# Two small table transfers moved from SyncE's queue to ScalarE's in a rotary-embedding kernel

## The chip, the cores and the metric

The kernel runs on one core of a Trainium2 chip. The metric is device time in microseconds (us), the median over executions. Ratios of two kernels are computed as the mean time of one kernel's fast runs over that of the other's of the same rounds, so they are not quite the ratio of the medians that are quoted beside them.

## The reference

```python
# x: [16, 512, 1024] float32, 16 heads of 64; cos, sin: [512, 32]
x = x.reshape(batch, seq, num_heads, head_dim)
x1, x2 = x[..., :32], x[..., 32:]
rotated = concatenate([x1 * cos - x2 * sin, x1 * sin + x2 * cos], axis=-1)
```

The input and the output are 33.55 MB each; the two tables are 64 KB each. There is little arithmetic for each byte.

## The kernel before

The batch is cut into eight tiles of 4 MB, each with 128 partitions of 8 x 1024 elements (eight slices "k" of 1024). Five tiles are held on chip at once. SyncE issues every transfer, in program order:

```python
FIRST = (3, 8)              # where the first tile's load is cut: k 0-2, then k 3-7
LAST_OUT = (4, 8)           # the last tile's store, likewise
...
    load(0, 0, FIRST[0])
    sin_sb = bp.tile([P, dim], FP32, name="b")[:PB, : KK * half]
    cos_sb = bp.tile([P, dim], FP32, name="b")[:PB, : KK * half]
    nc.sync.dma_start(out=sin_sb, in_=sin_v)
    nc.sync.dma_start(out=cos_sb, in_=cos_v)
    for lo, hi in zip(FIRST, FIRST[1:]):
        load(0, lo, hi)
    for t in range(1, BUFS):
        load(t)
```

PE then spreads the tables over 128 partitions, and VectorE (DVE in the profile) prepares them. Nothing of the main work can start earlier, because each main operation reads a table:

```python
    nc.tensor.matmul(out=sin_t, lhsT=spread, rhs=sin_sb, start=True, stop=True)   # L104
    nc.tensor.matmul(out=cos_t, lhsT=spread, rhs=cos_sb, start=True, stop=True)   # L105
    nc.vector.tensor_scalar_mul(out=sns[:, :, 0, :], in0=sin_k, scalar1=-1.0)     # L107
    nc.vector.tensor_copy(out=sns[:, :, 1, :], in_=sin_k)                         # L108
    ...
    for t in range(NT):            # main work: VectorE products and sums, GpSimd products,
        ...                        # PE and ScalarE for two of eight k
        nc.vector.tensor_tensor(out=pairs(ps), in0=pairs(rc), in1=cos_b(...), op=ALU.mult)  # L171
```

L171 is the first main operation of VectorE.

Of the kernel before, what the change touches and what calls it, by code (L numbers as in the profile page):

```python
# [27 lines left out]
def kernel(  # L28
# [13 lines left out]
    nc = tc.nc  # L42
# [12 lines left out]
    cos_v = cos.rearrange("(p k) j -> p (k j)", k=KK)  # L55
    sin_v = sin.rearrange("(p k) j -> p (k j)", k=KK)
# [22 lines left out]
    load(0, 0, FIRST[0])  # L79
    sin_sb = bp.tile([P, dim], FP32, name="b")[:PB, : KK * half]  # L80
    cos_sb = bp.tile([P, dim], FP32, name="b")[:PB, : KK * half]
    nc.sync.dma_start(out=sin_sb, in_=sin_v)
    nc.sync.dma_start(out=cos_sb, in_=cos_v)
    for lo, hi in zip(FIRST, FIRST[1:]):
        load(0, lo, hi)
    for t in range(1, BUFS):
# [27 lines left out]
    def cos_b(k, n):  # L114
        c = cos_t[:, k * half : (k + 1) * half]
        return bass.AP(tensor=c.tensor, offset=c.offset, ap=[c.ap[0], [0, n], [1, half]])
# [17 lines left out]
    def pairs(r):  # L134
        return r.rearrange("p (a j) -> p a j", j=half)
# [21 lines left out]
    for t in range(NT):  # L157
        xt = tiles[t]
        for k in range(KK):
# [6 lines left out]
            if k in PE_ROWS[t % 2]:  # L166
                parts = []
                for c in range(0, dim, BANK):
# [3 lines left out]
                        out=pairs(ps), in0=pairs(rc), in1=cos_b(k, BANK // half), op=ALU.mult  # L172
# [51 lines left out]
```

## Time and profile before

| | before |
|---|---|
| time, median of 3 runs | 162.77 us (162.58 to 162.78) |
| span of the profiled run | 160.8 us |
| VectorE busy | 141.4 us, 88% |
| transfers | 67.26 MB, packets on 97.9% of 16 engines' span |
| sine, cosine table: issue to landing | 6.5, 6.3 us |
| first main VectorE operation | at 10.90 us |
| last store issued | at 152.14 us |

Two rows compete for being the bound: VectorE, which never stops once it has started, and the transfers, which never stop at all.

### The profile page before, as it was taken

Reading aid. Unit: us, or ns where it says so; the run is one execution under the profiler, and the core shown is the slowest. Engines: PE = TensorE matmul, PEld = TensorE weight load, DVE = VectorE, ACT = ScalarE, POOL = GpSimd, SP = SyncE. Lnnn points to the kernel's source line nnn. Section 1 sums busy time; section 2 is a strip of 40 time slices with the busy share of each in tenths; the row PEclk is TensorE's granted clock in tenths of the full one; section 3 lists DMA queues with packets and bytes.
Section 4 is the critical chain, followed back from the end, with each engine's and each line's share of the span. In section 5 each row is a group of like instructions: output and inputs, shape, how many; then the busy total and the mean of one; then the engine's idle time right before and its main releaser. Section 6 shows DMA issues by size and latency. Waiting matters only on the chain. (4 is left out here: it accounts for less than half of the span.)

```text
span 160.8 us, 524 instructions
## 1 busy us (share of the span) xinstructions
PE 62.3 (39%) x71; PEld 20.0 (12%) x71; DVE 141.4 (88%) x142; ACT 20.0 (12%) x33; POOL 130.3 (81%) x62
## 2 busy tenths in 40 slices
PE   3045380546217260708035440918053721735000
PEld 0022020202011110202020200211020201111000
DVE  1059999999999999999999999999999999999800
ACT  0110220021102020111102020112002110202000
POOL 1039999999999999999999899999999799950000
PEclk9999958576956755595555555555955585587655
DMA  5999999999999999999999999999999999999994
GB/s 186 395 423 463 408 481 416 391 497 416 391 489 416 402 416 481 408 391 505 399 399 481 424 399 475 424 408 432 465 399 432 465 408 432 457 416 408 428 428 179
DMA packets 2754, 67.26 MB, mean 418 GB/s; under 512 B 320, under 2 KB 448, under 8 KB 448
## 3 DMA queue, kind: packets, MB, share of 16 engines
q1 hardware_dynamic: 2752, 67.24, 97.9%
q14 instruction: 2, 0.02, 0.0%
HBM read 33.69 MB, written 33.55 MB: 418 GB/s over the span
## 5 line engine op out<-in xcount | busy, mean ns | idle before, releaser
L165 POOL TENSOR_TENSOR b<-xt,sns 128x1024 f32<-128x1024 f32 x56 | 129.6, 2358 | 11.8 <-DVE sns L108 9.4
L183 DVE TENSOR_TENSOR pd<-xt,tab 128x1024 f32<-128x1024 f32 x48 | 58.1, 1225 | 0.8
L145 DVE TENSOR_TENSOR xt<-pd,b 128x1024 f32<-128x1024 f32 x48 | 58.4, 1218 | 0.0
L178 PE MATMUL ps<-xt,ident 128*128 128x512 f32 x32 | 29.5, 1077 | 48.6 <-issue 38.1
L178 PE MATMUL ps<-b,ident 128*128 128x512 f32 x32 | 29.4, 1073 | 29.8 <-DVE ps L171 27.1
L179 ACT COPY xt<-ps 128x512 f32<-128x512 f32 x32 | 18.7, 585 | 120.3 <-PE ps L178 120.3
L171 DVE TENSOR_TENSOR ps<-xt,tab 128x512 f32<-128x512 f32 x32 | 20.6, 688 | 0.0
L178 PEld LDWEIGHTS ps<-xt,ident 128*128 128x128 f32 x32 | 9.4, 324 | 68.2 <-issue 63.6
L178 PEld LDWEIGHTS ps<-b,ident 128*128 128x128 f32 x32 | 9.2, 316 | 49.7 <-issue 25.6
L176 DVE TENSOR_TENSOR xt<-xt,tab 128x1024 f32<-128x1024 f32 x8 | 9.8, 1221 | 0.4
L107 DVE TENSOR_SCALAR sns<-tab 128x256 f32<-128x256 f32 x1 | 0.4, 424 | 8.2 <-PE tab L105 8.2
L104 PE MATMUL tab<-b,spread 64*128 64x256 f32 x2 | 1.2, 696 | 5.1 <-DMA b<-in_sin_dram 5.1
L179 ACT ACT_TABLE_LOAD x1 | 1.3, 1283 | 7.3 <-DMA xt<-in_x_dram 7.3
L95 PE MATMUL ps<-zero 128*128 128x512 bf16 x3 | 1.5, 626 | 1.2 <-DVE zero L92 1.2
L104 PEld LDWEIGHTS tab<-b,spread 64*128 64x128 f32 x2 | 0.5, 307 | 6.0 <-issue 6.0
L105 PE MATMUL tab<-b,spread 64*128 64x256 f32 x2 | 1.1, 631 | 0.0
L92 DVE MEMSET zero<- 128x256 uint32 x1 | 0.3, 272 | 0.9 <-PEq L205 0.9
L105 PEld LDWEIGHTS tab<-b,spread 64*128 64x128 f32 x2 | 0.7, 333 | 0.2
L103 DVE COPY spread<-ident 64x64 f32<-64x64 f32 x2 | 0.3, 184 | 0.2 <-POOL ident masks.py:199 0.2
L95 PEld LDWEIGHTS <-zero 128*128 128x128 bf16 x3 | 0.3, 124 | 1.5 <-DVE zero L92 1.2
masks.py:197 POOL MEMSET ident<- 128x128 f32 x1 | 0.2, 205 | 0.3 <-POOLq L205 0.3
L108 DVE COPY sns<-tab 128x256 f32<-128x256 f32 x1 | 0.4, 414 | 0.0
(6 smaller groups left out, 0.9 us busy)
## 6 DMA issues: line engine op xcount, KB each, us to landing
xt<-in_x_dram SPq DMA_DIRECT2D x7, 4096.0 KB, 29.1
out_dram<-xt SPq DMA_DIRECT2D x7, 4096.0 KB, 23.6
out_dram<-xt SPq DMA_DIRECT2D x2, 2048.0 KB, 8.1
xt<-in_x_dram SPq DMA_DIRECT2D x1, 2560.0 KB, 11.5
xt<-in_x_dram SPq DMA_DIRECT2D x1, 1536.0 KB, 6.5
b<-in_sin_dram SPq DMA_DIRECT2D x1, 64.0 KB, 6.5
b<-in_cos_dram SPq DMA_DIRECT2D x1, 64.0 KB, 6.3
```

What stands on the lines that cost most here:

```text
L95: nc.tensor.matmul(out=ps, lhsT=zero[:, :P], rhs=zero, start=True, stop=True)
L104: nc.tensor.matmul(out=sin_t, lhsT=spread, rhs=sin_sb, start=True, stop=True)
L105: nc.tensor.matmul(out=cos_t, lhsT=spread, rhs=cos_sb, start=True, stop=True)
L107: nc.vector.tensor_scalar_mul(out=sns[:, :, 0, :], in0=sin_k, scalar1=-1.0)
L108: nc.vector.tensor_copy(out=sns[:, :, 1, :], in_=sin_k)
L145: nc.vector.tensor_tensor(out=r, in0=ps, in1=b, op=ALU.add)
L165: nc.gpsimd.tensor_tensor(out=halves(b), in0=swapped(r, nh), in1=over_heads(sk), op=ALU.mult)
L171: nc.vector.tensor_tensor(out=pairs(ps), in0=pairs(rc), in1=cos_b(k, BANK // half), op=ALU.mult)
L176: nc.vector.tensor_tensor(out=halves(r), in0=halves(r), in1=swapped_signed(k), op=ALU.mult)
L178: nc.tensor.matmul(out=ps, lhsT=ident, rhs=rhs, start=False, stop=True, skip_group_check=True)
L179: nc.scalar.copy(out=rc, in_=ps)
L183: nc.vector.tensor_tensor(out=pairs(ps), in0=pairs(r), in1=cos_b(k, 2 * nh), op=ALU.mult)
```

## The change

The intent is to free SyncE of two issues and to let the tables arrive on a queue of their own, beside the first piece of x instead of behind it.

```diff
-    nc.sync.dma_start(out=sin_sb, in_=sin_v)
-    nc.sync.dma_start(out=cos_sb, in_=cos_v)
+    nc.scalar.dma_start(out=sin_sb, in_=sin_v)
+    nc.scalar.dma_start(out=cos_sb, in_=cos_v)
```

Nothing else changes: the order of the other instructions is the same on each engine.

## The prediction

> **What bounds the kernel now.** I read the page's busy shares first, then the chain that ended last, then the transfers, because the first two and the third give different answers. VectorE (DVE) is the busiest compute engine, and the chain that ended last is made of its work:
>
> ```profile
> PE 62.3 (39%) x71; PEld 20.0 (12%) x71; DVE 141.4 (88%) x142; ACT 20.0 (12%) x33; POOL 130.3 (81%) x62
> ...
> DMA  5999999999999999999999999999999999999994
> ...
> q1 hardware_dynamic: 2752, 67.24, 97.9%
> ...
> DVE 10%; DVEq 1%; issue 1%
> ```
>
> That fits a VectorE bound: it starts late and then never stops. But the transfer row is at 9 from the second slice to the last but one, and the one queue's packets fill 97.9% of the time of 16 DMA engines. Two chains therefore run side by side over nearly the whole span. The table of windows shows which of them has room (columns: window, its length, busy time of PE, PEld, DVE, ACT, POOL with counts, granted clock, DMA share, GB/s):
>
> ```profile
> 0.00:1.50 1.50, 0.31 (x1) 0.13 (x2) 0.43 (x3) 0.00 (x0) 0.70 (x6) 1.00 0.00 0
> 1.50:2.50 1.00, 1.00 (x3) 0.15 (x1) 0.13 (x2) 0.00 (x0) 0.00 (x0) 1.00 1.06 209
> 2.50:20.00 17.50, 5.79 (x9) 2.34 (x8) 10.01 (x13) 2.45 (x3) 9.31 (x5) 1.00 0.99 415
> 20.00:60.00 40.00, 18.21 (x20) 5.67 (x20) 39.69 (x39) 5.85 (x10) 40.00 (x18) 0.68 1.01 433
> 60.00:100.00 40.00, 14.68 (x16) 4.71 (x16) 39.60 (x40) 4.68 (x8) 39.56 (x18) 0.54 1.00 433
> 100.00:140.00 40.00, 18.76 (x20) 5.87 (x20) 39.61 (x39) 5.60 (x10) 38.27 (x17) 0.59 1.00 433
> 140.00:150.00 10.00, 3.58 (x4) 1.17 (x4) 9.90 (x11) 1.42 (x3) 2.50 (x2) 0.83 0.98 424
> 150.00:158.00 8.00, 0.00 (x0) 0.00 (x0) 2.06 (x2) 0.00 (x0) 0.00 (x0) 0.51 1.00 430
> ```
>
> The DMA share is 0.98 to 1.06 in every window from 1.5 to 158 us, and the rate in the long windows is 433 GB/s each time, whether loads or stores are moving. The transfer engines have no hole to fill. As a check: 67.26 MB at 433 GB/s is 155.3 us; with 1.5 us before the first packet and about 2.8 us after 158 that is 159.6 of the 160.8 us span, and the slow first slices (186 and 395 GB/s) account for most of the missing 1.2 us. So **the transfers bound the kernel**, and VectorE keeps pace just behind them.
>
> How close is it? The last store, 2 MB, is issued when VectorE is done:
>
> ```profile
> 152.14 0.33 SPq L77 DMA_DIRECT2D out_dram<-xt  x1
> ...
> out_dram<-xt SPq DMA_DIRECT2D x2, 2048.0 KB, 8.1
> xt<-in_x_dram SPq DMA_DIRECT2D x1, 1536.0 KB, 6.5
> b<-in_sin_dram SPq DMA_DIRECT2D x1, 64.0 KB, 6.5
> b<-in_cos_dram SPq DMA_DIRECT2D x1, 64.0 KB, 6.3
> ```
>
> It lands at about 152.14 + 8.1 = 160.2 us. The first load (1536 KB, 1.57 MB, 3.6 us at 433 GB/s) met an empty queue and took 6.5 us, so start and landing cost some 2.9 us on an idle queue. A 2 MB store (2.10 MB, 4.8 us) would then take about 7.7 us on an idle queue; 8.1 leaves an estimated 0.4 us of backlog in front of it. VectorE is thus some 0.4 us ahead of running the queue dry at the end: balanced, with the transfers deciding.
>
> **What the Trainium skill says.** "DMA: Bandwidth & Descriptors", section "Issuing engines are not separate DMA queues": transfers from ScalarE and SyncE run on the same 16 engines and interleave; another issuer only saves the sequencer's issue time. The kernel before uses one queue, so its trace can't show the interleaving. The same page, "Queues, rings and completion order": each engine alternates between the rows it has work for, packet by packet, draining a packet of several descriptors before it switches. No run here shows that yet; it is why I expect the tables not to wait behind all of the queued loads. The same page, "Where 436 GB/s comes from", puts the ceiling at 435.2 GB/s; the 433 GB/s of the long windows agrees. "Perfetto Trace Analysis", section "DMA Instruction — HWDGE (DVE, Sync)": the profiled interval of such an instruction leaves out the movement of data. The trace agrees: 0.52 us of issue for the sine table, 6.5 us to landing.
>
> **The change part by part.** *Removed from SyncE:* two issues of 0.52 and 0.58 us. The next load is issued at 2.36 us now, about 1.2 us earlier after. Worth nothing: the first load's 1.57 MB keep the engines busy until past 5 us, so that load waits in the queue either way. *Added to ScalarE:* the same two issues, some 1.1 us, at the start. Its first work needs PE, at 15.79 us, so this costs nothing. No other engine's order changes, and bytes and packets stay the same.
>
> *Moved: when the tables land.* Today they lie in the queue behind the first load:
>
> ```profile
> 7.77 1.19 PE L104 MATMUL tab<-b,spread 64*128 64x256 f32 x2 [5.12 <-DMA b<-in_sin_dram]
> ...
> 9.85 0.42 DVE L107 TENSOR_SCALAR sns<-tab 128x256 f32<-128x256 f32 x1 [8.22 <-PE tab L105]
> ...
> 10.90 1.29 DVE L171 TENSOR_TENSOR ps<-xt,tab 128x512 f32<-128x512 f32 x2
> ```
>
> Sine lands at 1.17 + 6.5 = 7.7 us, cosine at 1.74 + 6.3 = 8.0, the first piece of x at 0.73 + 6.5 = 7.2. From the sine landing, four matmul passes and three VectorE operations take 3.2 us to the first real operation at 10.90. On a queue of their own the tables are issued at about 0.7 us; alternating with the first load I expect them by 4 to 6.5 us. The first piece of x then decides: at 7.2 us, plus up to 0.3 for the 0.13 MB of tables moved in front of its end. VectorE's main work starts at 7.5 to 9.5 us, my middle 8.0, about 3 us earlier. GpSimd gains less: its third operation needs the load issued at 2.36 us, which lands at 2.36 + 11.5 = 13.9 as before, so it waits there.
>
> *What of it reaches the end.* VectorE works without a break at 17.6 us a tile (stores are issued 17.6 us apart), so it should finish near 149 instead of 152. Its last store is then issued with 3 us more in front of it, and leaves the transfer engines no earlier. Sum: issue 0, VectorE 3 us hidden, transfers 0 to 0.3 us better (packets without a hole at the start) or worse (small packets between large ones). Predicted **162.6 us**.
>
> **The rivals.** (1) *VectorE is the bound*: for it speak the chain and that VectorE is never idle after 10 us. Then all 3 us reach the end: 159.6 us, 1.9% faster. Against it: no window has a transfer share that could rise; to finish 3 us sooner the same bytes would have to move at over 440 GB/s. (2) *The tables are served late*, because SyncE's queue holds five tiles of loads by 5 us and wins the arbitration. Should they come after all of that (20 MB, 48 us), the time would be some 200 us. The skill's alternation speaks against it; a mild form (1 us later than now) costs about 0.6 us after the 0.4 of backlog. (3) *Mixing small packets between large ones costs transfer time*: 1 KB rows between 12 KB rows, eight per engine (64 rows of two tables over 16 engines); if each cost 0.2 us, my guess, that is 1.6 us and 164.2. Nothing in this trace shows it. (4) *A new order of stores and loads*: earlier stores could change which loads queue ahead. But the last load is issued at 82.23 us when the third store has landed, which the transfers decide, and the next store waits behind it on SyncE in either kernel.
>
> **Range and chances.** The spread of the times before is 0.2 us. Rivals 1 to 3 in part give 162.1 to 163.3 us as the 8-in-10 range. Faster by over 2% needs 159.5 us, more than even all of rival 1: 0.02. Slower by over 2% needs 166.0, which only a bad rival 2 or 3 gives: 0.02. Within 2%: 0.96.
>
> **What would show it.** Right: the first VectorE table operation near 5 to 8 us and the first main one at 7.5 to 9.5; the last store issued near 149 us, with its time to landing grown from 8.1 to about 11; the DMA share still at 1.00 in all windows and a span within 0.5 us of 160.8. Wrong: a lower share or rate in the first 10 us (rival 3), tables landing after 8 us (rival 2), or a rate above 433 GB/s in the long windows with an earlier end (rival 1). The prediction fails if the transfer share of 1.00 hides engines that wait rather than move.

## The result, and the profile after

The changed kernel takes 164.67 us (median of 6 runs, 164.07 to 165.28) against 162.68 (6 runs, 162.51 to 162.92): a ratio of 1.0122, 95% interval 1.0088 to 1.0156. It is 2.0 us slower. That is inside 2%, but outside the range of 162.1 to 163.3 us.

The page's queues and issues of the kernel after (columns of the last lines: out<-in, issuing engine, count, KB, us from issue to landing):

```profile
q1 hardware_dynamic: 2592, 67.11, 97.0%
q10 hardware_dynamic: 160, 0.13, 0.2%
...
out_dram<-xt SPq DMA_DIRECT2D x2, 2048.0 KB, 7.2
...
b<-in_sin_dram ACTq DMA_DIRECT2D x1, 64.0 KB, 7.3
b<-in_cos_dram ACTq DMA_DIRECT2D x1, 64.0 KB, 10.9
```

ScalarE's queue, q10, carries 160 packets: 128 table rows of 1 KB and 32 far smaller ones, which is ten for each of 16 engines. The tables are issued sooner (0.73 and 1.29 us instead of 1.17 and 1.74), and yet the cosine table lands at 1.29 + 10.9 = 12.2 us instead of 8.0. What waits for it is in the timeline of the kernel after, from 8 to 16 us (start, duration, engine, line, operation, and in brackets the idle time before and what ended it):

```profile
8.15 1.19 PE L104 MATMUL tab<-b,spread 64*128 64x256 f32 x2 [5.50 <-DMA b<-in_sin_dram]
...
12.29 0.50 PEld L105 LDWEIGHTS tab<-b,spread 64*128 64x128 f32 x2 [3.67 <-DMA b<-in_cos_dram]
...
13.54 0.42 DVE L107 TENSOR_SCALAR sns<-tab 128x256 f32<-128x256 f32 x1 [11.92 <-PE tab L105]
...
14.60 1.29 DVE L171 TENSOR_TENSOR ps<-xt,tab 128x512 f32<-128x512 f32 x2
```

L171 starts at 14.60 us instead of 10.90, so VectorE is 3.7 us late. It then works without a break exactly as before, and the last store is issued 3.66 us later, at 155.80 instead of 152.14.

```profile
155.80 0.33 SPq L77 DMA_DIRECT2D out_dram<-xt  x1
```

That the end moved by 2.7 us only (span 163.5 instead of 160.8) is seen in the table of windows of the kernel after (window, length, busy time of PE, PEld, DVE, ACT, POOL, clock, DMA share, GB/s):

```profile
100.00:140.00 40.00, 14.98 (x17) 5.01 (x18) 39.52 (x40) 4.68 (x8) 37.81 (x17) 0.69 1.00 420
140.00:150.00 10.00, 5.94 (x8) 1.86 (x7) 9.93 (x11) 1.76 (x3) 6.18 (x3) 0.67 0.89 380
150.00:158.00 8.00, 0.86 (x2) 0.00 (x0) 5.69 (x5) 0.59 (x1) 0.00 (x0) 0.50 0.99 422
```

The DMA share falls to 0.89 between 140 and 150 us, where it was 0.98 before. The queue runs dry while it waits for VectorE's next store, and the last store meets less work ahead of it (median landing of the two last stores 7.2 us instead of 8.1). The last store alone, in the kernel before and in the kernel after:

```profile
out_dram<-xt SPq DMA_DIRECT2D x1, 2048.0 KB, 7.6
```

```profile
out_dram<-xt SPq DMA_DIRECT2D x1, 2048.0 KB, 6.6
```

It takes 6.3 us in the four one-queue kernels below in which VectorE comes 2 us late or more. So some 1.3 us of backlog (transfers still queued in front of the last store) stood there before, and 0.3 us is left after. The spans agree: 3.66 us of later issue less 1.0 us of shorter landing is 2.7 us, and the spans are 163.5 and 160.8 us. The backlog is nearly used up, and VectorE sets the end.

The transfers were slower as well, in two stretches where stores give way to loads and loads to stores. Before and after:

```profile
78.00:86.00 8.00, 3.13 (x4) 1.18 (x4) 7.97 (x8) 0.59 (x1) 8.00 (x4) 0.50 1.02 438
106.00:114.00 8.00, 3.75 (x4) 1.18 (x4) 7.93 (x9) 1.17 (x2) 7.65 (x4) 0.59 1.03 442
```

```profile
78.00:86.00 8.00, 2.25 (x3) 0.34 (x1) 7.90 (x9) 1.17 (x2) 8.00 (x5) 0.50 0.98 385
106.00:114.00 8.00, 4.19 (x6) 1.34 (x5) 7.97 (x9) 1.48 (x3) 7.74 (x4) 0.71 0.98 373
```

That is some 2.3 us at 433 GB/s. It is not the second queue (one queue with the tables behind six k, below, has 381 and 381 GB/s there), and it does not set the end, since the queue still runs dry after it. Why it happens is open; with 16 memsets, below, both stretches have 442 GB/s.

How did a queue of its own make the tables later? Here is what moved in two stretches of the kernel after (queue, packets, MB, share of 16 engines), first from 0 to 5 us:

```profile
q1 hardware_dynamic: 93, 1.14, 66.6%
```

and then from 7 to 11.2 us:

```profile
q1 hardware_dynamic: 79, 1.62, 96.0%
q10 hardware_dynamic: 79, 0.07, 4.7%
```

In the first stretch q10 has no line at all: some six packets of x pass on each engine before a single row of the tables moves. In the second, the two queues move the same number of packets. They take turns, one for one, but a packet of x here holds 20 KB and a packet of a table 1 KB. On one queue, the tables had gone through in one block.

### The profile page after: what moved, and what is told of

Read it like the earlier page. It is cut to its first block, busy times and chain, and to the rows that moved or that the text cites. A ratio compares the mean times of both kernels' runs of the same rounds, so it can differ in the third digit from the quotient of the medians.

```text
span 163.5 us, 523 instructions
## 1 busy us (share of the span) xinstructions
PE 62.6 (38%) x71; PEld 19.9 (12%) x71; DVE 141.4 (86%) x142; ACT 20.0 (12%) x33; POOL 130.3 (80%) x62
## 5 line engine op out<-in xcount | busy, mean ns | idle before, releaser
L171 DVE TENSOR_TENSOR ps<-xt,tab 128x512 f32<-128x512 f32 x32 | 20.5, 687 | 0.0
## 6 DMA issues: line engine op xcount, KB each, us to landing
b<-in_cos_dram ACTq DMA_DIRECT2D x1, 64.0 KB, 10.9
```

## The experiments

**Theory A.** Only VectorE's late start costs. The tables are late because their few small packets take turns with large ones; beyond a small backlog, each us of VectorE's start is a us of the end. **Theory B.** The second queue costs by itself, because small packets between large ones waste transfer time. **Rival C.** VectorE alone is the bound, so that an earlier start would also have gained. **Rival D.** The second queue has a fixed delay, whatever moves beside it.

### The changed kernel again, in two more sessions

No edit.

> The changed kernel once more, unchanged, for a second trace. Theory A (the tables' few small packets take turns with the large ones of the loads, one for one, so the cosine table lands late, VectorE starts late, and the end follows VectorE): cosine lands near 12 us, first main VectorE operation near 14.6 us, 164.1 to 165.3 us. The six runs so far fall into two groups, 164.1 and 165.2; if A is right the group should follow the landing of the cosine table. Theory B (mixing small packets into large ones costs transfer time for its own sake): the DMA rate of the first 20 us is below that of the kernel before, by the time lost.

> The changed kernel on the same chip as the three runs beside it, for a comparison free of differences between chips: 164.1 to 165.3 us, VectorE's table operation near 13.4 us.

It took 164.22 us (164.15 to 164.74; before beside it 162.66) and 164.91 us (164.77 to 165.59; before 162.63). L171 started at 14.35 and 14.42 us, and the cosine table took 10.7 and 10.8 us to land. The late landing repeats. Theory B's sign did not come: from 2.5 to 20 us the rate is 416, 416 and 415 GB/s in the three traces of the changed kernel, and 415 before. The spread of about 1 us between sessions does not follow the landing of the tables, as A expected; that differs by 0.25 us at most. It follows the last store, which took 6.6, 6.3 and 7.1 us to land where the profiled executions took 165.28, 164.74 and 165.59 us. So in two of the three some backlog was left, 0.3 and 0.8 us: the transfers were late too. Why they differ between sessions is open.

### As late, but on one queue

```diff
-FIRST = (3, 8)
+FIRST = (6, 8)      # in the kernel before: the tables queue behind twice as much of x
```

> The kernel before (tables on SyncE, one queue) with the first piece of x grown from 3 to 6 of 8, so the tables queue behind 3.15 MB instead of 1.57 MB: 1.57 MB at 433 GB/s is 3.6 us, so VectorE starts near 14.5 us, as late as in the changed kernel, without a second queue. Theory A (only the late start of VectorE costs): the same time as the changed kernel, 164.2 to 165.3 us, last store issued near 155.7 and landed about 7 us later. Theory B (it is the second queue or its mixing that costs): 162.5 to 163.0 us.

Its first main VectorE operation:

```profile
14.52 1.29 DVE L171 TENSOR_TENSOR ps<-xt,tab 128x512 f32<-128x512 f32 x2
```

The time was 165.25 us (164.90 to 165.38; before 162.52; ratio 1.0168, interval 1.0151 to 1.0185). All transfers are on SyncE's queue, the tables go through in a block, and the cost is no less than the changed kernel's. This speaks for A and against B.

### VectorE late, transfers untouched

```diff
+    scratch = fixed.tile([P, BANK], FP32)
+    for i in range(24):                     # 24, 19, 16 and 14 in the four runs
+        nc.vector.memset(scratch, 0.0)
     nc.tensor.matmul(out=sin_t, lhsT=spread, rhs=sin_sb, start=True, stop=True)
```

> The kernel before, transfers untouched and one queue, with 24 idle memsets (0.48 us each) on VectorE ahead of its table operations, so that these start near 13.4 us, as late as in the changed kernel. Theory A (the whole cost of the change is VectorE's late start): within 0.5 us of the changed kernel beside it, 164.1 to 165.3 us. Theory B (part of the cost comes from the second queue): 163 us or less, or clearly under the changed kernel.

> The same with 19 memsets: table operations near 11.0 us, 1.1 us later than before. If the backlog at the end is 0.4 to 0.9 us (my estimate, and the one from the shorter landing of the last store in the changed kernel), the time grows by 0.2 to 0.7 us only: 162.7 to 163.3 us. Without any backlog it would grow by 1.1 us: 163.7 us.

These two missed their aim: a memset of the same tile takes 0.66 us in a row, not 0.48, so VectorE came later than meant. In the timelines of the two kernels, with 24 and 19 memsets:

```profile
18.20 1.29 DVE L174 TENSOR_TENSOR ps<-xt,tab 128x512 f32<-128x512 f32 x2
```

```profile
14.91 1.29 DVE L174 TENSOR_TENSOR ps<-xt,tab 128x512 f32<-128x512 f32 x2
```

They took 168.86 us (168.85 to 168.87) and 165.53 us (165.40 to 165.96), with 162.63 before beside them. Between the two, 3.29 us of start cost 3.33 us of time: a slope of one. But 19 memsets no longer said anything about the backlog, so two more runs were made around the point where the line should meet the floor.

> 14 memsets of 0.66 us: first main VectorE operation near 11.6 us, 0.7 us later than before. Backlog of 1.1 us: no change, 162.5 to 162.8 us. Backlog of 0.4 us: 162.9 to 163.0. No backlog: 163.3.

> 16 memsets: first main VectorE operation near 12.9 us, 2.0 us later than before. Line of slope one through the two delayed kernels: 163.5 us. Backlog of 0.4 us from the kernel before: 164.2. No backlog: 164.6.

With 16 memsets L171 started at 12.94 us and the time was 163.31 us (163.30 to 163.32; before 162.54), close to the 163.5 of the line. With 14 it started at 11.62 us, and the time was 163.45 us with a wide spread (162.90 to 164.28): 0.9 us over the kernel before, where I expected no change, and no better than the later start. So the line holds from 2 us of delay on. Nearer to the floor the time scatters, and a delay of 0.7 us was not free. In its profiled execution the last store took 7.2 us, so the transfers still set the end there.

### One table on each queue

```diff
 nc.scalar.dma_start(out=sin_sb, in_=sin_v)
-nc.scalar.dma_start(out=cos_sb, in_=cos_v)
+nc.sync.dma_start(out=cos_sb, in_=cos_v)
```

> Sine on ScalarE's queue, cosine on SyncE behind the first piece of x. Theory A: the sine table has only the first five turns and lands near 8.0 us, cosine near 7.7; VectorE starts near 11.2 us, 0.3 us later than before, inside the 0.4 to 0.9 us of backlog: 162.5 to 163.1 us. Rival (any transfer on the second queue costs): 164 us or more.

162.66 us (162.44 to 162.84) against 162.52: ratio 1.0005, interval 0.9990 to 1.0020. L171 started at 10.85 us. A second queue with half of the packets costs nothing, where the rival asked for 164 us or more. The sine table landed at 0.73 + 6.8 = 7.5 us. It is the second table, whose turns come after the first one's and beside packets of 20 KB, that made the change slow.

### Smaller and larger packets beside the tables

```diff
-FIRST = (3, 8)
+FIRST = (1, 2, 3, 4, 5, 6, 7, 8)   # small rows: all eight k of the first tile at 4 KB a row
+FIRST = (1, 2, 3, 8)               # three small: k 0 to 2 at 4 KB, the rest at 20 KB
+FIRST = (8,)                       # large rows: 32 KB
```

All three are edits of the changed kernel, with the tables on ScalarE.

> The changed kernel with the first tile loaded in eight pieces of one k each (4 KB rows instead of 12 and 20 KB), tables still on ScalarE. Theory A (one small packet per packet of the other queue): a turn costs some 0.16 us instead of 0.47 to 0.83, so ten turns end several us earlier: both tables landed by 6 to 7 us, VectorE starts at 8 to 10 us, time 162.5 to 163.2. Rival (the second queue is slow by itself, whatever the size of the packets beside it): cosine still lands near 12 us, time 164 to 165.3.

> The changed kernel with only the first three k of the first tile in pieces of 4 KB rows, the rest as it was (20 KB rows). Theory A: the turns of both tables fall mostly beside small packets; cosine lands by 7 to 8.5 us, VectorE starts at 9 to 11 us, not later than before; time 162.4 to 163.1 us. The transfers are the floor, so it can't be much under the kernel before. If it is at 164 or more, the size of the packets beside the tables is not what decides.

> The changed kernel with the first tile loaded in one piece (32 KB rows). Theory A with sizes from the two traces of the changed kernel: some six packets of the loads pass on each engine first (1.75 + 0.6 + 6 x 1.21 = 9.6 us), then up to nine turns at 1.21 us: cosine lands at 18 to 21.5 us, VectorE starts at 20.5 to 24 us, time 171 to 175 us. Rival (a fixed delay of the second queue, about 11 us for the cosine table): it lands near 12 us, VectorE waits for x alone, which lands near 13 us, and the time is about 165 us.

| rows beside the tables | sine, cosine: issue to landing | L171 starts | time (before beside it) |
|---|---|---|---|
| 4 KB | 4.2, 5.3 us | 8.98 us | 163.12 (162.66) |
| 4 KB, then 20 KB | 4.3, 5.4 us | 9.06 us | 162.75 (162.63) |
| 12 KB, then 20 KB (the change) | 7.3, 10.9 us | 14.60 us | 164.67 (162.68) |
| 32 KB | 10.5, 15.4 us | 19.07 us | 169.35 (162.52) |

Rival D is out: the tables' landing follows the size of the rows beside them. With 32 KB rows the turns are exact, from 4.7 to 15.1 us:

```profile
q1 hardware_dynamic: 144, 4.19, 99.7%
q10 hardware_dynamic: 144, 0.13, 3.8%
```

144 packets each are nine turns per engine in 10.4 us, or 1.16 us a turn. Two expectations failed in part. The large rows came out at 169.35 (two executions) instead of 171 to 175 us, because only 32 packets of x, two per engine, passed before the first table row, where I had assumed six. And the small rows are not strictly one for one: from 3.3 to 6 us,

```profile
q1 hardware_dynamic: 233, 0.82, 86.0%
q10 hardware_dynamic: 158, 0.13, 18.6%
```

The x queue moved 1.5 packets for each table packet there.

### The tables issued first

```diff
+    tiles[0] = xp.tile([P, F], FP32, name="xt")
+    nc.vector.memset(tiles[0][:, :512], 0.0)      # holds back the first load (changed kernel)
     load(0, 0, FIRST[0])
```

> The changed kernel with the first load held back by a VectorE memset of 512 columns of its tile, some 0.6 us, so that the table transfers are issued first. Theory A with a head start (what is queued first on an engine is served first; the loads got some 3 us of it in the changed kernel): sine lands near 4 us, cosine by 5 to 7, VectorE starts near 8 to 9 us, time 162.7 to 163.4 (up to 0.5 us lost by the transfers that start later). Rival (ScalarE's queue needs over 4 us from issue to its first packet anyway): sine lands near 8, cosine near 12, time 164.3 to 165.5.

The first load was issued at 1.43 us, after both tables (0.73 and 1.29). The sine table then landed in 2.2 us, and the cosine in 7.2 us, at 8.5: later than A's 5 to 7, earlier than the rival's 12. From 0 to 3 us:

```profile
q1 hardware_dynamic: 15, 0.18, 34.5%
q10 hardware_dynamic: 80, 0.07, 8.2%
```

All 80 packets of the sine table pass almost alone; the cosine table, issued 0.14 us ahead of x, is already caught by the turns. With 0.7 us of lead the sine table does not wait, so a fixed delay of ScalarE's queue is out, and the 3 us without a table row are not a must. What decides who goes first is not shown: in the changed kernel both queues were issued within 0.01 us of each other. VectorE started at 10.85 us, as in the kernel before and 2 us later than A said, and the time was 163.73 us (163.35 to 164.35; before 162.66), 0.3 us over A's range. Here the transfers set the end: x's first load was issued 0.7 us later, and the median landing of the two last stores grew to 9.1 us.

### VectorE early

```diff
+    nc.sync.dma_start(out=sin_sb, in_=sin_v)      # kernel before, tables ahead of x
+    nc.sync.dma_start(out=cos_sb, in_=cos_v)
     load(0, 0, FIRST[0])
```

and, as the second edit of the kernel before, `FIRST = (1, 3, 8)`: one k, the tables, then two more.

> Both table transfers on SyncE, ahead of the first piece of x; ScalarE issues none. Theory A with the transfers as the floor: sine lands near 3.5 us, cosine near 4, x near 7.8; VectorE starts near 8 us and ends near 149.3, but the time stays at 162.5 to 163.0 because the DMA engines have no hole to fill. Rival (VectorE alone is the bound, so each us of its start counts): 159.6 to 160.0 us.

> The kernel before with the first piece of x cut to 1 of 8, then the tables, then two more pieces, all on SyncE. Tables land near 5.5 us, VectorE starts near 8.6 us, 2.3 us earlier than before, and the first packet of x still moves at 1.74 us. Theory A with the transfers as the floor: 162.4 to 162.9 us, last store issued near 150 with about 10 us to landing. Rival (VectorE alone is the bound): 160.4 us.

L171 started at 8.64 and 8.58 us, 2.3 us earlier than before, and the times were 164.12 us (163.73 to 164.85; before 162.66) and 164.65 us (164.55 to 165.10; before 162.52). Rival C is out: it asked for 160.4 or less. But both are also slower than the floor that I expected. The last stores were issued at 150.00 and 150.06 us and took 12.0 and 12.3 us (median of the two last stores), so the transfers set the end, and they were slower. The windows of the kernel before (left out columns are as above):

```profile
1.50:5.00 3.50, 1.15 (x3) 0.15 (x1) 0.13 (x2) 0.00 (x0) 0.00 (x0) 1.00 0.96 330
47.00:55.00 8.00, 3.69 (x4) 1.17 (x4) 7.97 (x9) 1.17 (x2) 8.00 (x5) 0.71 0.97 411
```

and of the kernel with one k ahead of the tables:

```profile
1.50:5.00 3.50, 1.32 (x4) 0.36 (x3) 0.12 (x2) 0.55 (x1) 0.00 (x0) 1.00 0.85 234
47.00:55.00 8.00, 4.19 (x6) 1.19 (x5) 7.97 (x9) 1.17 (x2) 8.00 (x5) 0.50 1.03 382
```

The DMA engines are less filled in the first 5 us, which is worth (0.96 - 0.85) x 3.5 = 0.4 us, and between 47 and 55 us, where loads give way to the first stores, the same share moves less, 382 instead of 411 GB/s, about 0.5 us at 433 GB/s. The rest, some 1.2 us, these windows do not show, but the landings place it in the same stretch: the fourth tile's load landed 0.8 us later than before (43.9 against 43.0), the fifth's 2.6 us (55.3 against 52.7), and no more was lost after that. Why the change-over is slower there was not tried.

### VectorE's delay and the cost, all kernels

VectorE's delay is the start of L171 less 10.90 us; the cost is the time less that of the kernel before in the same session.

| kernel | delay | cost | delay less cost |
|---|---|---|---|
| one queue, one k ahead of the tables | -2.32 | 2.13 | |
| one queue, tables first | -2.26 | 1.46 | |
| small rows, ScalarE | -1.92 | 0.46 | |
| three small, ScalarE | -1.84 | 0.12 | |
| tables issued first, ScalarE | -0.05 | 1.07 | |
| one table on each queue | -0.05 | 0.14 | |
| 14 memsets | 0.72 | 0.91 | |
| 16 memsets | 2.04 | 0.77 | 1.27 |
| **the change, second session** | 3.45 | 1.56 | 1.89 |
| **the change, last session** | 3.52 | 2.28 | 1.24 |
| one queue, tables behind six k | 3.62 | 2.73 | 0.89 |
| **the change, first session** | 3.70 | 1.99 | 1.71 |
| 19 memsets | 4.01 | 2.90 | 1.11 |
| 24 memsets | 7.30 | 6.23 | 1.07 |
| large rows, ScalarE | 8.17 | 6.83 | 1.34 |

From 2 us of delay on, the last column is 0.9 to 1.3 us on one queue, whatever made VectorE late; that fits the 1.3 us of backlog in front of the last store. The change has 1.2 to 1.9, so it costs no more than its delay does on one queue, and nothing is left over for B. Without a delay no such line holds: there the transfers set the end, and some kernels lose up to 2.1 us in them. No version tried beat the kernel before; one table on each queue and three small pieces equal it within the noise.

## Why the prediction was wrong

**The bound.** Right. The transfers set the end before. Where VectorE started earlier (four kernels) nothing was gained, as "VectorE 3 us hidden" said. But two of these lost 1.5 and 2.1 us in the transfers, where the sum allowed for 0.3.

**The issues.** Right. Two fewer on SyncE and two more on ScalarE had no effect of their own that any run shows: with both moved and the first rows small, the time is 162.75 against 162.63 us; with one moved, 162.66 against 162.52.

**The landing of the tables: the step that failed.** The prediction said "alternating with the first load I expect them by 4 to 6.5 us". They landed at 8.0 and 12.2 us, the cosine 4.2 us later than before instead of 1.5 to 4 us earlier. Two things were taken wrongly. I let the alternation begin at once; in the trace 93 packets of x passed first, and no table row moved before 5 us. And I let an engine take several table rows in a turn, as the skill describes a packet; in the trace a turn is one row, ten turns are needed per engine, and most of the cosine table's fall beside rows of 20 KB at about 0.85 us each (79 turns on 16 engines in 4.2 us).

**VectorE's start.** "7.5 to 9.5 us" became 14.60, by the failed step alone: from the cosine landing on, the chain took 2.4 us, against 2.9 from 8.0 us to 10.90 before.

**The backlog: mis-sized.** I estimated 0.4 us; the last store shows 1.3, and the one-queue runs with a late VectorE 0.9 to 1.3. Two readings were off. The 8.1 us is the median of the two last stores, where the last one took 7.6. And I had taken 7.7 us for a 2 MB store on an idle queue from a load's fixed 2.9 us, where it takes 6.3. The error worked in favour of the change: with 0.4 us it would have cost 3.1 us.

**The rivals.** Rival 2, tables served late, was the one that came true, in the mild form. Its reckoning (delay less backlog) was sound; its delay of 1 us was 3.5 to 3.7. I gave it little weight because of the skill's alternation, without working out how many turns the tables need and how long each lasts, though all the sizes were in the profile: eight rows per engine beside rows of 0.47 to 0.8 us each. Rival 3, whose figures I did work out, would have given nearly the right time for a wrong reason; the one-queue run with the same delay and cost excludes it as the cause. Rival 4 did not occur: in the changed kernel the third store, three loads and the fourth store are still issued in that order, though the transfers between them were slower (windows above).

**The range.** 162.1 to 163.3 us left room for a landing 1 us late, not for 3.5.

## What to carry to other kernels

In these runs a second queue was no fast lane: its packets took turns with those of the first, so a small transfer in many small rows, beside a queue full of large ones, landed after about (its packets per engine) x (the time of one large packet), plus what passed before it. Behind a short load on the same queue it was there sooner. Before a transfer is moved, look at who waits for it and count its turns. And where two chains are balanced, measure how much slack the hidden one has: here some 1.3 us of 162.

## What the Trainium skill lacked or had wrong

- "DMA: Bandwidth & Descriptors", section "Queues, rings and completion order", lets an engine drain a packet of several descriptors (it calls some 9 to 17 typical) from one row before it switches. Between SyncE's and ScalarE's queues here the turns were one row each: 79 packets against 79 (20 KB and 1 KB), 144 against 144 (32 KB and 1 KB); beside 4 KB rows 233 against 158.
- The same page says nothing of a lead: with both queues issued at 0.73 us, 93 packets of x (12 KB) moved before 5 us and none of the tables; with 32 KB rows 32 packets before 4.7 us, with 4 KB rows 93 before 3.3 us. Issued 0.7 us ahead of x, the sine table had no such wait and landed in 2.2 us. What sets the lead is open.
- The same page, "Issuing engines are not separate DMA queues", is right that a second issuer adds no bandwidth (404 GB/s from 1.5 to 20 us in both kernels). It lacks the warning that it can delay a small transfer: cosine landing at 12.2 us on the second queue, 8.0 us on the first.
